# Delta heads with raw keys and queries: the lengths move into beta, the values and the head norm; the decay comes from one F32 tile; the score tiles are placed first

## The chip, the cores and the metric

The kernel runs on one core of a Trainium2 chip. The metric is the device time of one execution in microseconds (us). Five engines work side by side, each through its own instructions in order: TensorE (PE, matrix products), VectorE (DVE), ScalarE (ACT), GpSimd (POOL) and SyncE (SP), whose queue here issues all loads and stores. Semaphores order the engines among each other.

## The reference

One layer of an encoder over 1024 tokens of width 1024: a mixer, a cross-attention into 256 memory tokens, and a SwiGLU block, each with RMS norms before and after it. The mixer has two halves that read the same projection. One is a windowed softmax attention. The other, which the change touches, is a gated delta rule with 4 heads of width 128, in both directions of time:

```python
q = _l2norm(q) * DN_HEAD_K ** -0.5          # _l2norm(x) = x * rsqrt(sum(x*x) + EPS)
k = _l2norm(k)
g = jnp.cumsum(g, axis=-1)                  # within a chunk
decay = exp(where(incl, g[..., :, None] - g[..., None, :], -inf))
kb = k * beta[..., None]
lower = where(strict, einsum('bhnid,bhnjd->bhnij', kb, k) * decay, 0.0)
sol = triangular_solve(lower + eye(c), concat([v * beta, kb * exp(g)]))
qk = einsum('bhnid,bhnjd->bhnij', q, k) * decay
# per chunk: v_new = u - w @ state; o = qg @ state + qk @ v_new; state = state * gl + kg.T @ v_new
o = o_fwd + o_bwd
o = o * rsqrt(mean(o * o, axis=-1, keepdims=True) + EPS) * g_out * silu(gate)
```

q, k and v are a centred 5-tap convolution and SiLU of projected columns. The kernel uses chunks of 128 tokens.

## The kernel before

The kernel is written against a tile framework. Each engine's order is set by a scheduler that plays the program on its own model of times: a ready instruction that stands earlier in the program goes first. Buffers come from pools, and a new tile waits for the last readers of the memory that it takes.

The mixer has three stages. ORDER_1 takes the delta heads 0 to 3: `delta_proj` (D) projects the key, query and value columns of a head. Each projection is 48 matmuls of 128x512 (line 259; activation and weight are split into a high and a low part, F32R tiles) and is then convolved: ACT copies the product out of PSUM, DVE adds four taps (line 284, tile `acc`, a ring of 3), ACT applies SiLU. `prep` (P) makes of a head what the recurrence needs, in two halves of four chunks that take turns. `base_inverse` (B) inverts, for two heads at once, the 32x32 diagonal blocks of I + lower on DVE, 30 steps of two instructions (lines 524 and 526), after it has loaded the blocks (tile `V`, four loads) and the beta rows.

A half of `prep` goes like this. POOL spreads the gate over a mask, once for the gate's high part and once for its low part and for both directions (`gm`, line 450), and four F32R matmuls (line 451) sum them to exponents, of which ACT makes the decay `E`. PE turns the key tile (line 441) into PSUM, ACT squares it and sums, POOL takes the power -1/2 (lines 159 and 160), DVE multiplies (line 466): a key of length one, token by token, in `kv`. The query goes the same way. The values are turned and copied (line 468). Then PE turns the normed keys and queries back (line 473), ACT copies them (line 474), `kv` is stored to `d_kv` as one block of 1 MB, and PE makes the score products key by key and key by query (line 481), which DVE multiplies with `E` out of PSUM (`U`, line 484, stored to `d_u`; `pc`, line 488). All these PSUM results come from one ring of five banks, `ps`. Beta is turned, stored to `d_beta` once for all heads and read by both base inverses.

ORDER_2 takes the two `levels` for each pair of heads (they read what the base inverse stored, multiply it up to 128x128 and store `Z`), the gates (G), the attention projections (A, V) and the first attention windows (W). Its pools `tw` and `tl_` lie where those of ORDER_1 were. ORDER_3 runs the two recurrences (`scan`), step by step, beside windows and the memory's keys and values (K, V). A step loads `kv` and `pz`. From the fifth step on, the two directions are added, squared and normed with the power on POOL (`rstd_of`) and scaled by the gate.

The rest (output projection, cross-attention, SwiGLU) is not touched.

## Time and profile before

| what | us |
|---|---|
| median of three runs (1584.72 to 1590.94) | 1587.42 |
| the profiled execution, its own time | 1588.8 |
| span of the profiled execution, first to last instruction | 1587.1 |
| delta heads (70 to 255 us): length of the stretch / PE busy in it | 185 / 170.5 |
| levels of heads 0 and 1, second base inverse (255 to 345 us) | 90 / 79.1 |
| levels of heads 2 and 3, first windows (345 to 405 us) | 60 / 55.3 |
| recurrences, windows, memory (405 to 570 us) | 165 / 152.9 |

The profile names an instruction by line, engine, operation and tiles; buffer numbers are left out. A matmul with F32 operands of 128 columns shows as two records, a transpose and an F32R matmul as one. A record of PE lasts longer than the time to the next one's start, because matmuls overlap; what one costs in a row is read from start to start. `PEclk` is the share of TensorE's full clock that was granted. "Waited for" gives total time, number of waits and the longest, and the engine and line that ended them.

### The profile page before, as it was taken

What the parts mean: (1) busy time and instruction counts of PE and PEld (TensorE: products, weight loads), DVE (VectorE), ACT (ScalarE), POOL (GpSimd) and SP (SyncE); (2) the same over time, 40 slices, a digit from 0 to 9 for tenths busy, and PEclk for the clock granted to TensorE, in tenths of its full rate; (3) what the DMA queues carried; (4) which work ended last, traced back from release to release, by engine and by line L of the source; (5) the groups of instructions that cost most, each with busy time, mean ns of one, the idle gap of its engine ahead of it and who ended that gap; (6) DMA issues with size and microseconds to landing.
All of it is one profiled execution on the core that took longest, in us unless ns stands there. A gap on an engine that the chain in (4) does not pass through costs nothing.

```text
span 1587.1 us, 21186 instructions
## 1 busy us (share of the span) xinstructions
PE 1505.9 (95%) x7514; PEld 1260.3 (79%) x7514; DVE 1059.3 (67%) x1616; ACT 762.4 (48%) x1523; POOL 497.4 (31%) x447
## 2 busy tenths in 40 slices
PE   6999889989799989999999999999999999999998
PEld 5877777868689967788888777888888888888786
DVE  6846887975678865444345549677768655596565
ACT  6556543238766685554335566322322332344532
POOL 2368644233134510243301140443434433100021
PEclk9999999989999999999999999999999999999999
DMA  6134148483998675455222254443335332853354
GB/s 207 42 118 129 41 153 226 113 206 103 283 289 284 191 251 206 146 186 157 69 72 79 90 186 140 128 154 127 118 118 166 100 100 100 292 206 112 107 171 161
DMA packets 252151, 242.97 MB, mean 153 GB/s; under 512 B 33528, under 2 KB 187021, under 8 KB 252045
## 3 DMA queue, kind: packets, MB, share of 16 engines
q1 hardware_dynamic: 252045, 241.62, 48.0%
q8 instruction: 59, 0.97, 0.3%
q14 instruction: 47, 0.39, 0.1%
HBM read 172.07 MB, written 66.88 MB: 151 GB/s over the span
## 4 chain that ended last, share of the span: by engine, by line
PE 67%; DVE 13%; DMA 7%; ACT 5%; issue 3%; POOL 3%; SPq 2%; DVEq 0%; POOLq 0%; ACTq 0%
PE pmg L1005 8%; PE pD L1180 7%; PE pE L1180 7%; PE pA L1180 6%; PE pcq L259 6%; PE pdX L1370 5%; PE pg L259 4%; PE pdA L1370 4%; PE pB L1180 4%; PE psc L777 3%; DVE acc L284 2%; PE pdD L1370 2%; DVE tmpb L524 2%; DVE A L526 2%; PE pcs L1086 1%
## 5 line engine op out<-in xcount | busy, mean ns | idle before, releaser
L102 ACT CAST whi<-wraw 128x1024 fp32r<-128x1024 f32 x108 | 113.3, 1050 | 161.5 <-PE pmg L1005 34.9
L103 POOL TENSOR_TENSOR wlo<-wraw,whi 128x1024 fp32r<-128x1024 f32 x48 | 119.7, 2494 | 193.9 <-ACT whi L102 171.4
L259 PE MATMUL pg<-hlo,whi 128*128 128x512 f32 x352 | 140.2, 399 | 0.0
L259 PE MATMUL pg<-hhi,whi 128*128 128x512 f32 x352 | 140.1, 399 | 0.1
L259 PE MATMUL pg<-hhi,wlo 128*128 128x512 f32 x352 | 139.9, 398 | 0.0
L103 DVE TENSOR_TENSOR wlo<-wraw,whi 128x1024 fp32r<-128x1024 f32 x60 | 74.5, 1244 | 79.4 <-ACT whi L102 75.1
L1005 PE MATMUL pmg<-whi,b 128*128 128x512 f32 x384 | 118.4, 394 | 2.6 <-ACT whi L102 2.2
L1180 PE MATMUL pA<-s,whi 128*128 128x512 f32 x352 | 109.6, 392 | 1.4 <-ACT m L1197 1.4
L284 DVE SCALAR_TENSOR_TENSOR acc<-cp,cols,acc 128x1024 f32<-128x1024 f32 x48 | 73.8, 1539 | 19.5 <-ACT acc L282 18.9
L1005 PEld LDWEIGHTS pmg<-whi,b 128*128 128x128 f32 x384 | 71.2, 188 | 17.9 <-ACT whi L102 2.7
L259 PEld LDWEIGHTS pg<-hhi,whi 128*128 128x128 f32 x352 | 67.1, 191 | 13.6 <-ACT hhi L102 0.4
L1257 POOL TENSOR_TENSOR act<-act,up 128x512 f32<-128x512 f32 x33 | 50.1, 1519 | 88.1 <-DVE up L1256 53.0
L259 PEld LDWEIGHTS pg<-hhi,wlo 128*128 128x128 f32 x352 | 67.1, 191 | 13.2
L259 PEld LDWEIGHTS pg<-hlo,whi 128*128 128x128 f32 x352 | 67.2, 191 | 13.1
L1370 PE MATMUL pdX<-dhl,whi 128*128 128x512 f32 x264 | 76.1, 390 | 1.5 <-ACT dhl L102 0.8
L1180 PEld LDWEIGHTS pA<-s,whi 128*128 128x128 f32 x352 | 65.3, 188 | 15.2 <-ACT m L1197 2.0
L1400 POOL TENSOR_SCALAR frs<-sq 128x1 f32<-128x1 f32 x8 | 11.9, 1497 | 195.7 <-ACT jk L1389 194.8
L1005 PE MATMUL pmg<-wlo,b 128*128 128x512 f32 x192 | 71.4, 391 | 0.0
L1180 PE MATMUL pA<-s,wlo 128*128 128x512 f32 x176 | 68.8, 392 | 1.9 <-DVE wlo L103 1.9
L102 ACT CAST whi<-araw 128x1024 fp32r<-128x1024 f32 (+1 forms) x36 | 35.4, 982 | 71.3 <-PE pdX L1370 27.6
L1229 POOL TENSOR_TENSOR sr<-wraw 128x512 f32<-128x512 f32 x22 | 29.2, 1328 | 126.4 <-DMA wraw<-in_w_gate_up_dram 125.6
L103 DVE TENSOR_TENSOR wlo<-araw,whi 128x1024 fp32r<-128x1024 f32 (+1 forms) x36 | 40.7, 1132 | 38.5 <-ACT whi L102 38.3
(409 smaller groups left out, 4230.3 us busy)
## 6 DMA issues: line engine op xcount, KB each, us to landing
wraw<-in_w_gate_up_dram SPq DMA_DIRECT2D x52, 512.0 KB, 3.9
kv<-d_kv SPq DMA_DIRECT2D x32, 512.0 KB, 6.7
wraw<-in_w_in_dram SPq DMA_DIRECT2D x22, 512.0 KB, 4.3
b<-in_w_down_dram SPq DMA_DIRECT2D x20, 512.0 KB, 7.0
araw<-d_as SPq DMA_DIRECT2D x20, 512.0 KB, 3.7
d_kv<-kv SPq DMA_DIRECT2D x8, 1024.0 KB, 7.2
pz<-d_pz SPq DMA_DIRECT2D x32, 256.0 KB, 6.0
wraw<-in_w_ckv_dram SPq DMA_DIRECT2D x16, 512.0 KB, 7.2
```

The lines of the kernel that those rows point to most:

```text
L102: nc.scalar.copy(hi, src)
L103: (eng or nc.vector).tensor_tensor(lo, src, f32(hi), ALU.subtract)
L259: nc.tensor.matmul(p_, w[:, k, :], ah[a][:, k, :], start=(k == 0 and i == 0), stop=(k == nk - 1 and i == 2))
L284: nc.vector.scalar_tensor_tensor(acc, cp[:, t:t + S], taps[t], acc, ALU.mult, ALU.add)
L524: nc.vector.tensor_tensor(tv, A[:, j + 1:, j:j + 1].to_broadcast([P, n, j]), A[:, j:j + 1, 0:j].to_broadcast([P, n, j]), ALU.mult)
L526: nc.vector.tensor_tensor(A[:, j + 1:, 0:j], A[:, j + 1:, 0:j], tv, ALU.add)
L777: nc.tensor.matmul(out[:, d, h, :], lt[:, d, h, :], rt[:, d, h, :], start=True, stop=True)
L1005: nc.tensor.matmul(pp[t], act[a][:, k, tt], w_[:, kk, :], start=(k == 0 and i == 0), stop=(k == KT - 1 and i == 2))
L1180: nc.tensor.matmul(out_, w[a][:, k, :], xx[b_][:, k, :], start=(start and k == 0 and i == 0), stop=(k == HK - 1 and i == 2), skip_group_ch ...
L1229: nc.gpsimd.tensor_tensor(s[0], b_[:, 0:HK], b_[:, HK:], ALU.add)
L1257: nc.gpsimd.tensor_tensor(o_, o_, up, ALU.mult)
L1370: nc.tensor.matmul(banks[t], a[:, k - k0, tt], w, start=(first and k == 0 and i == 0), stop=(k == NB - 1 and i == 2), skip_group_check=not ...
```

## The change

Keys and queries stay raw. With x the sum of a key's squares plus EPS, the key by key products carry the lengths of two keys; beta is divided by x, the values are multiplied by the root of x, so that the recurrence gives the same result. The query's length and its 128 cancel in the head norm but for EPS, which is scaled by the query's squares instead (`epsq`).

So the two norm multiplies and the two turns back go. The raw key and query tiles (width by token, as they come from the convolution) are stored from `acc` straight to their places in `d_kv`, are the operands of the score products, and are still turned for their squares. `acc` becomes a ring of 5. The decay's exponents come from two F32 matmuls on the unsplit gate in place of four F32R ones. Beta is stored per pair of heads, after the second head's keys are squared. The norm of the recurrence's output takes one more POOL instruction. A line takes the eight score tiles as the first of the pool `tw`.

```diff
-    mU_r = sm.tile([P, P], F32R, name="mU_r")
-    mL_r = sm.tile([P, P], F32R, name="mL_r")
+    mU_s = sm.tile([P, P], F32, name="mU_s")
+    mL_s = sm.tile([P, P], F32, name="mL_s")
...
-        acc = tcv.tile([P, S], F32, tag="acc", name="acc", bufs=3)
+        acc = tcv.tile([P, S], F32, tag="acc", name="acc", bufs=5)
...
-    pt = small()
-    nc.tensor.transpose(pt[0:64, 0:P], beta.rearrange("p d h c -> p (d h c)"), ident)
-    bT = sm.tile([64, P], F32, name="bT")
-    nc.scalar.copy(bT, pt[0:64, 0:P])
-    nc.sync.dma_start(d_beta, bT)
+    phalf = sm.tile([P, 32], F32, name="phalf")
+    nc.gpsimd.memset(phalf, 0.5)
...
+    def beta_rows(g):
+        hs = slice(2 * g, 2 * g + 2)
+        bp = sm.tile([P, 2, 2, NT], F32, name=f"bp{g}")
+        xi = sm.tile([P, 2, NT], F32, name=f"xi{g}")
+        nc.vector.reciprocal(xi, xk[:, hs, :])
+        nc.vector.tensor_tensor(bp, beta[:, :, hs, :], bc(xi, 1, (P, 2, 2, NT)), ALU.mult)
+        pt = small()
+        nc.tensor.transpose(pt[0:32, 0:P], bp.rearrange("p d h c -> p (d h c)"), ident)
+        bT = t2.tile([32, P], F32, tag="bT", name="bT", bufs=1)
+        nc.scalar.copy(bT, pt[0:32, 0:P])
+        nc.sync.dma_start(d_beta[g], bT)
...
+        for src, i in ((kc, 2), (qc, 3)):
+            nc.sync.dma_start(d_kv[g][:, :, hh, i].rearrange("c p n -> p c n"), src.rearrange("p (c n) -> p c n", c=NT))
...
-                for part in (ghi, glo):
-                    gm = t2.tile([P, 4, P], F32R, tag="gm", name="gm")
-                    nc.gpsimd.tensor_tensor(gm, bc(part[:, d, h, c4], 2, (P, 4, P)), bc(cm[mi], 1, (P, 4, P)), ALU.mult)
-                    nc.tensor.matmul(pa, ml, gm.rearrange("p c n -> p (c n)"), start=(n == 0), stop=(n == 3))
-                    n += 1
+                gm = t2.tile([P, 4, P], F32, tag="gm", name="gm")
+                nc.gpsimd.tensor_tensor(gm, bc(G[:, d, h, c4], 2, (P, 4, P)), bc(cm[mi], 1, (P, 4, P)), ALU.mult)
+                nc.tensor.matmul(pa, ml, gm.rearrange("p c n -> p (c n)"), start=(d == 0), stop=(d == 1))
...
-                rs = t2.tile([P, 4], F32, tag="rs4", name="rs4", bufs=4)
-                rstd_of(rs, ss, n, e)
-                nc.vector.tensor_tensor(kv[:, :, i, :], pk, bc(rs, 2, (P, 4, P)), ALU.mult)
+            kv = t2.tile([P, 4, 2, P], F32, tag="kv", name="kv")
             yield
-            nc.scalar.copy(kv[:, :, 1, :], turned(vc))
-            for i, o in ((0, 2), (3, 3)):
-                yield
-                p_ = small()
-                for j in range(4):
-                    nc.tensor.transpose(p_[:, j * P:(j + 1) * P], kv[:, j, i, :], ident)
-                nc.scalar.copy(kv[:, :, o, :], p_.rearrange("p (c n) -> p c n", c=4))
-            nc.sync.dma_start(d_kv[g][c4, :, hh].rearrange("c p s n -> p c s n"), kv)
+            pk = turned(kc)
+            nc.scalar.copy(kv[:, :, 0, :], pk)
+            ss = squares(pk, False)
+            nc.gpsimd.tensor_scalar(xk[:, h, c4], ss, EPS, None, ALU.add)
+            nc.gpsimd.tensor_tensor(rootk[:, h, c4], xk[:, h, c4], phalf[:, 0:4], ALU.pow)
+            if hh and b:
+                beta_rows(g)
...
-                    nc.tensor.matmul(p_[:, j, :], kv[:, j, 2, :], kv[:, j, i, :], start=True, stop=True)
+                    o = (4 * b + j) * P
+                    nc.tensor.matmul(p_[:, j, :], kc[:, o:o + P], src[:, o:o + P], start=True, stop=True)
...
+            nc.gpsimd.tensor_scalar(epsq[:, g, :, 1 - b, hh], squares(turned(qc), b == 0), P * EPS, P * EPS * EPS,
+                                    ALU.mult, ALU.add)
+            yield
+            nc.vector.tensor_tensor(kv[:, :, 1, :], turned(vc), bc(rootk[:, h, c4], 2, (P, 4, P)), ALU.mult)
+            nc.sync.dma_start(d_kv[g][c4, :, hh, 0:2].rearrange("c p s n -> p c s n"), kv)
...
+    tw.tile([P, 384], F32, tag="sc", name="sc", bufs=8)
...
-            rstd_of(rs.rearrange("p d h -> p (d h)"), ss.rearrange("p d h -> p (d h)"), 1.0 / P, EPS)
+            nc.gpsimd.tensor_scalar(rf, sf, 1.0 / P, None, ALU.mult)
+            nc.gpsimd.tensor_tensor(rf, rf, epsq[:, g, step - NT // 2].rearrange("p d h -> p (d h)"), ALU.add)
+            nc.gpsimd.tensor_tensor(rf, rf, mhalf[:, 0:4], ALU.pow)
```

The scheduler orders the engines anew. Three places follow; a number behind a tile's name is that of its buffer.

The first is PE in the `prep` of head 1. Rows of line 259 are projections. Before, the turns back (line 473) stand between projections, and the score products (line 481) come after them:

```order
L473 MATMUL ps_1210<-ident_68,kv_1109 128x128 x4
L259 MATMUL pg_1354<-hhi1_227,whi_1349 128x512
L259 MATMUL pg_1354<-hlo1_228,whi_1349 128x512
L473 MATMUL ps_1216<-ident_68,kv_1125 128x128 x4
L259 MATMUL pg_1354<-hhi1_227,wlo_1350 128x512
L473 MATMUL ps_1222<-ident_68,kv_1109 128x128 x4
L473 MATMUL ps_1229<-ident_68,kv_1125 128x128 x4
L259 MATMUL pg_1422<-hhi0_141,whi_1418 128x512
```

After, in the same `prep` (line 435 turns the beta rows, 486 makes the score products, 452 turns the raw queries for their squares):

```order
L435 MATMUL ps_1107<-ident_68,bp0_1103 32x128
L486 MATMUL ps_1112<-acc_899 128x128 x4
L486 MATMUL ps_1120<-acc_899 128x128 x4
L486 MATMUL ps_1128<-acc_968,acc_899 128x128 x4
L486 MATMUL ps_1139<-acc_968,acc_899 128x128 x4
L452 MATMUL ps_1150<-ident_68,acc_968 128x128 x4
L259 MATMUL pg_1273<-hhi0_142,whi_1269 128x512
L259 MATMUL pg_1273<-hlo0_143,whi_1269 128x512
L452 MATMUL ps_1165<-ident_68,acc_968 128x128 x4
```

The sixteen score products now stand in one piece, and before the query is turned. Over the four heads, from the first `gm` product to the first level, the 540 projection matmuls stand in 18 stretches, where they stood in 44. The score products of head 1 come after 194 of the 540, where 236 stood ahead of the first of them.

The second is DVE inside the first base inverse, at the `prep` of head 2. Before (524 and 526 are a step of the inverse, 284 a tap, 484 and 488 take the score products out of PSUM):

```order
L524 TENSOR_TENSOR tmpb_2070<-A_2066 128x238
L284 SCALAR_TENSOR_TENSOR acc_1797<-cp_1794,cols_71,acc_1797 128x1024
L526 TENSOR_TENSOR A_2066<-A_2066,tmpb_2070 128x14x17
L484 TENSOR_TENSOR U_1640<-ps_1635,E_1514 128x512
L488 TENSOR_TENSOR pc_1648<-ps_1643,E_1498 128x512
```

After (536 and 538 are the step, 489 is `U`):

```order
L538 TENSOR_TENSOR A_1911<-A_1911,tmpb_1915 128x22x9
L489 TENSOR_TENSOR U_1466<-ps_1461,E_1414 128x512
L536 TENSOR_TENSOR tmpb_1915<-A_1911 128x210
L538 TENSOR_TENSOR A_1911<-A_1911,tmpb_1915 128x21x10
L489 TENSOR_TENSOR U_1474<-ps_1469,E_1424 128x512
L536 TENSOR_TENSOR tmpb_1915<-A_1911 128x220
```

The two `U` of head 2 have moved from behind steps 16 and 17 of the base inverse to behind steps 9 and 10.

The third is SP's queue at the start of the recurrences. Before, the last loads of the first stretch are:

```order
L785 DMA kv_4185<-d_kv1_100 128x1024
L786 DMA pz_4184<-d_pz11_104 128x512
L785 DMA kv_4418<-d_kv0_99 128x1024
L786 DMA pz_4417<-d_pz00_101 128x512
L676 DMA kraw_4236<-d_k_97 64x1024
L125 DMA wraw_4383<-in_w_ckv_dram 128x8x128
```

After (798 loads `kv`, 799 `pz`, 679 stores a window, 688 loads the attention's keys, 635 a window's queries):

```order
L799 DMA pz_4278<-d_pz10_103 128x512
L798 DMA kv_4279<-d_kv1_100 128x1024
L679 DMA d_mix_113<-ao_3345 64x4x128
L688 DMA kraw_4082<-d_k_97 64x1024
L125 DMA wraw_4229<-in_w_ckv_dram 128x8x128
L635 DMA qr_3872<-d_q_96 64x4x128 x2
```

Eight loads of `kv` and seven of `pz` now stand ahead of the attention's keys (`kraw`) and of the memory's weights, where five and five stood.

## The prediction

> **What bounds the kernel now.** I read the page's head first, then the stages, then who PE waited for, then the order of time at the places that the change touches.

> ```profile
> span 1587.1 us, 21186 instructions
> ...
> PE 1505.9 (95%) x7514; PEld 1260.3 (79%) x7514; DVE 1059.3 (67%) x1616; ACT 762.4 (48%) x1523; POOL 497.4 (31%) x447
> ...
> PE 67%; DVE 13%; DMA 7%; ACT 5%; issue 3%; POOL 3%; SPq 2%; DVEq 0%; POOLq 0%; ACTq 0%
> ```

> PE sets the end: it is busy for 95% of the span and is two thirds of the chain that ended last. A microsecond is worth something if it is taken from PE's work or from its waits. The change lies in the mixer, whose stages are (columns: stretch, length, busy time of PE, PEld, DVE, ACT, POOL with counts, granted clock, DMA share, GB/s):

> ```profile
> 70.00:255.00 185.00, 170.54 (x878) 141.69 (x878) 133.51 (x148) 99.92 (x253) 116.25 (x107) 0.98 0.41 121
> 255.00:345.00 90.00, 79.05 (x409) 67.36 (x409) 78.52 (x143) 22.79 (x53) 29.57 (x22) 0.93 0.63 166
> 345.00:405.00 60.00, 55.26 (x314) 47.59 (x313) 35.73 (x88) 45.26 (x100) 19.67 (x19) 0.96 0.47 136
> 405.00:570.00 165.00, 152.93 (x1125) 142.42 (x1126) 129.48 (x336) 115.06 (x306) 62.73 (x65) 0.97 0.82 253
> ```

> The delta heads take 185 us with 14.5 us in which PE stands; the next 90 us have 11 us of standing, with DVE at 87%. From 60 to 420 us PE waited for (engine, line, releaser: total, times, longest):

> ```profile
> PE ps L441 <- DVE kv L466: 5.5, 3, 2.6
> PE ps L583 <- DVE L L576: 5.0, 1, 5.0
> PE ps L473 <- DVE kv L466: 3.8, 3, 1.7
> PE ps L451 <- POOL gm L450: 2.9, 3, 1.5
> PE ps L574 <- DVE Z L606: 2.4, 1, 2.4
> PE ps L441 <- ACT E L454: 2.0, 1, 2.0
> ```

> Lines 441 and 473 wait for the norm multiply that the change takes out, 9.3 us in all. The 583 and 574 waits come in the levels, when DVE still works on the second base inverse.

> **PE's work.** What an instruction costs in a row is read from start to start (start, length, engine, line, operation, shape, count):

> ```profile
> 243.16 0.60 PE L473 MATMUL ps<-ident,kv 128*128 128x128 f32 x4
> 243.51 0.48 PE L259 MATMUL pg<-hhi,wlo 128*128 128x512 f32 x1
> 243.83 0.39 PE L259 MATMUL pg<-hhi,whi 128*128 128x512 f32 x1
> 244.06 0.40 PE L259 MATMUL pg<-hlo,whi 128*128 128x512 f32 x1
> ...
> 244.75 3.74 PE L481 MATMUL ps<-kv 128*128 128x128 f32 x32
> 248.25 0.48 PE L259 MATMUL pg<-hlo,whi 128*128 128x512 f32 x1
> ```

> Four turns take 243.51 - 243.16 = 0.35 us. Eight halves lose eight turns back each, 64 turns: 64 x 0.35 / 4 = 5.6 us less. An F32R matmul of 512 columns takes 244.06 - 243.83 = 0.23 us; eight halves lose four: 32 x 0.23 = 7.4 us less. In their place come 16 F32 matmuls of 512 columns, a shape that the trace does not have. Sixteen F32 matmuls of 128 columns (32 records) take 248.25 - 244.75 = 3.50 us, 0.219 each. If the time goes by columns, 512 take 4 x 0.219 = 0.875 us, 14.0 us in all, 6.6 more than the F32R ones. The lower end: F32 matmuls of 32 columns cost as much as those of 128, so what is paid there may be the weights and not the columns:

> ```profile
> 261.71 1.87 PE L583 MATMUL ps<-m,L 128*128 128x32 f32 x16
> 263.41 0.47 PE L259 MATMUL pg<-hhi,wlo 128*128 128x512 f32 x1
> ```

> Eight of them in 263.41 - 261.71 = 1.70 us, 0.21 each. Then two records of 512 columns would cost what two F32R matmuls do, 0.46 us, and the decay nothing more than before. I take 0.875: the same type on the same engine is the nearest row. Two turns of beta in place of one: 0.1 us. Work in sum: -5.6 + 6.6 + 0.1 = **+1.1 us** (-5.5 to +1.1); PE has no less to do than before.

> [...]

> Fewer pieces: the first projection after small matmuls takes 243.83 - 243.51 = 0.32 us to the next, 0.09 above 0.23. The order has 44 stretches of projections in the four heads before and 18 now: 26 x 0.09 = **-2.3 us** (0 to -2.3).

> **PE's waits in the heads.** The norm multiply goes, and with it 9.3 us; of the 2.9 us for `gm` I take half away, since POOL makes two of these tiles per half and not four: **-10.8 us** (-14.2 to 0). The wait for `E` stays. New waits come in, because five banks of `ps` must still be emptied: the turned query needs a bank that the squares on ACT release or `U` on DVE. The costs beside PE (busy us, mean ns):

> ```profile
> L463 ACT ACTIVATE jk<-ps 128x128 f32<-128x128 f32 x64 | 17.2, 333 | 0.0
> L474 ACT COPY kv<-ps 128x512 f32<-128x512 f32 x16 | 9.0, 603 | 1.5 <-PE ps L473 1.4
> L466 DVE TENSOR_TENSOR kv<-ps,rs 128x512 f32<-128x512 f32 x16 | 10.9, 687 | 17.4 <-POOL rs L160 15.7 <-POOL cp L276 0.9 <-POOL cp L277 0.7
> L160 POOL TENSOR_TENSOR rs<-rs,mhalf 128x4 f32<-128x4 f32 x16 | 19.1, 1200 | 0.5
> L646 POOL TENSOR_TENSOR es<-prm,m 128x4 f32<-128x4 f32 x9 | 2.2, 244 | 15.5 <-DVE m L636 8.8 <-PE ptw L657 6.4
> ```

> ACT loses two copies per half and DVE one multiply of 0.687 us (8 x 0.687 = 5.5 us), POOL half of its powers. I give the new waits 4 us, one per head, the size of two multiplies plus two copies (2.6 us) and a little queueing; between 0 and 9.3, the wait that the same banks cost until now. **+4 us**.

> **The base inverses.** They run on DVE and are hindered by POOL (`gm`, line 450):

> ```profile
> 226.39 0.24 DVE L526 TENSOR_TENSOR A<-A,tmpb 128x84 f32<-128x84 f32 x1
> 226.77 1.04 POOL L450 TENSOR_TENSOR gm<-ghi,C 128x512 fp32r<-128x512 f32 x1
> 226.92 0.96 DVE L526 TENSOR_TENSOR A<-A,tmpb 128x58 f32<-128x58 f32 x1
> 227.92 0.93 DVE L524 TENSOR_TENSOR tmpb<-A 128x30 f32<-128x30 f32 x1
> ```

> A step that takes 0.24 us takes 0.95 beside a `gm`: each of the eight `gm` that go in heads 2 and 3 frees up to 0.7 us of DVE there, 5.6 us at most. Besides, `U` of head 1 is made 42 projections earlier in PE's order, 42 x 0.23 = 9.7 us, and the first inverse starts from it (above its rows that of the taps, which stand between its steps):

> ```profile
> L284 DVE SCALAR_TENSOR_TENSOR acc<-cp,cols,acc 128x1024 f32<-128x1024 f32 x48 | 73.8, 1539 | 19.5 <-ACT acc L282 18.9
> 162.37 3.95 DVE L515 SCALAR_TENSOR_TENSOR A<-V,bB 64x1024 f32<-64x1024 f32 x1 [8.97 <-DMA V<-d_u]
> 229.19 2.12 DVE L528 TENSOR_TENSOR V<-A,bB 128x1024 f32<-128x1024 f32 x1
> 267.65 2.00 DVE L515 SCALAR_TENSOR_TENSOR A<-V,bB 64x1024 f32<-64x1024 f32 x1 [3.04 <-DMA V<-d_u]
> ```

> The second inverse should then start some 10 us earlier against PE, and the levels' waits of 5.0 and 2.4 us mostly go: **-6 us** (-7.4 to 0). Late next is the beta row: squares, reciprocal, turn, copy, store, load. It runs beside `U`, its store (6.1 us) and the `V` loads, so I cost it at nothing; without that cover a store and a load would follow that of `U`, up to 6.1 us each by the row of `d_u` below. The granted clock was 0.98 and 0.93 in these stretches: 2% of 185 and 7% of 90 us are 10 us, of which I take a fifth, **-2 us** (0 to -6).

> **Stores and loads.** `d_kv` was written as 1 MB and is now written as half a MB from `kv` and twice half a MB per head from `acc`:

> ```profile
> d_kv<-kv SPq DMA_DIRECT2D x8, 1024.0 KB, 7.2
> d_u<-U SPq DMA_DIRECT2D x8, 256.0 KB, 6.1
> kv<-d_kv SPq DMA_DIRECT2D x32, 512.0 KB, 6.7
> ```

> The bytes are the same, and DMA is 41% busy there: nothing. SP is in order, though: behind the store of a raw key, which waits for SiLU, stand weight loads; these are needed some 100 projections (23 us) later, so that is nothing too. At the start of the recurrences three `kv` and two `pz` more stand ahead of the attention's keys and the memory's weights: 3 x 0.52 + 2 x 0.26 = 2.1 MB, at 253 GB/s 8.3 us. PE waits there already, in the chain for these loads:

> ```profile
> 409.44 7.22 DMA pz<-d_pz
> 416.68 11.60 DMA kv<-d_kv
> ```

> I take **+2.5 us** (0 to 8.3), since the scan's own loads come sooner for it. One more POOL instruction of 0.244 us per norm is hidden for a step; the last ones are not: **+0.3 us**. The score tiles' place lets other tiles take memory that is free earlier or later; values no longer lie where the base inverse was, and I cost it at nothing.

> **Sum** against the profiled execution: 1588.8 + 1.1 - 2.3 - 10.8 + 4 - 6 - 2 + 2.5 + 0.3 = 1575.6 us. That execution is 1.4 above the median, so 1574.2 against 1587.4: 1574, or -0.8%. About 0.5%, 8 us, is what a measurement of this kernel tells from no change.

> **Rivals.** *DVE holds PE in the heads (slower).* `U` of head 2 now stands behind step 9 of the first inverse. If that inverse doesn't start earlier (the fourth `V` load is queued on SP behind the stores of `kv`), DVE is late for PE: 162.4, plus 6 us for the inverse's first two instructions, nine steps at twice some 0.6 us and four taps at 1.5 us make 185, while PE, which has lost some 10 us of waits, would be there at about 174. That is 11 us in head 2, and as much in head 3, whose beta row stands on DVE behind the inverse's end at 231. With 22 us in place of 4, and without the levels' 6, the sum is 1588.8 + 1.1 - 2.3 - 10.8 + 22 - 2 + 2.5 + 0.3 = 1599.6, 1598 against the median. From 11 us of new waits on the kernel gains nothing, from 19 it is slower by over 0.5%. Against it: DVE has less to do and `U` comes earlier.

> *The gain is given back (no change).* PE has no less work. If the levels still wait for the second inverse, the clock stays and the recurrences wait for all 8.3 us of loads, the sum is 1588.8 + 1.1 - 2.3 - 10.8 + 4 + 8.3 + 0.3 = 1589.4, 1588 against the median. For it: the later stages start from DVE's inverse and from loads, not from PE's work in the heads.

> *More goes.* The F32 matmuls cost the lower end (-5.5), all 14.2 us of waits go with 2 us new, then the levels' 7.4 and 6 us of clock, and the loads are hidden: 1588.8 - 5.5 - 2.3 - 14.2 + 2 - 7.4 - 6 + 0.3 = 1555.7, 1554 against the median.

> **Chances.** Forecast (1566 to 1579) 0.51; more (below) 0.12; given back (1580 to 1595) 0.19; DVE holds PE (above) 0.18. So faster by over 0.5% 0.63, within it 0.19, slower 0.18. The range reaches half way into "more" and to the price of the slower rival: 1559 to 1598, with some 0.06 left out below and 0.13 above.

> **What would show it.** The wait of lines 441 and 473 for `kv` gone from PE's list, waits for `U`, `pc` or squares of about 4 us in its place; `gm` products of 0.875 us; the first inverse starting before 155 us; the level of head 2 on PE before 322 us where it came at 330; the 405 to 570 stretch as long as before, 10 to 15 us earlier. Waits above 15 us for DVE in the heads, or an inverse that starts at 162, would make the forecast wrong.

## The result: no change

The changed kernel takes 1586.85 us (median of 20 runs, 1581.95 to 1591.49), the kernel before 1587.01 us (20 runs, 1582.54 to 1590.94). The ratio is 0.9996 (95% interval 0.9988 to 1.0004). 1574 us was forecast. The profiled execution of the changed kernel is the fastest of its 20 (1581.95 us), that of the kernel before lies 1.8 us above its median: the 7 us between the two pages are scatter for the most part.

The head of the changed kernel's page, and its chain by engine:

```profile
span 1580.1 us, 21010 instructions
...
PE 1503.9 (95%) x7451; PEld 1256.4 (80%) x7451; DVE 1047.9 (66%) x1609; ACT 748.8 (47%) x1504; POOL 462.1 (29%) x432
...
PE 74%; DVE 11%; DMA 6%; ACT 4%; issue 2%; SPq 1%; POOL 1%; DVEq 0%; POOLq 0%; ACTq 0%
```

VectorE has lost 11 us, ScalarE 14, GpSimd 35; PE 2. By stage, in the columns of the prediction's table:

```profile
70.00:255.00 185.00, 171.83 (x831) 137.90 (x829) 128.02 (x143) 91.72 (x237) 86.33 (x84) 0.98 0.44 123
255.00:345.00 90.00, 79.88 (x405) 68.09 (x405) 77.56 (x154) 25.55 (x60) 27.93 (x22) 0.91 0.64 160
345.00:405.00 60.00, 56.70 (x319) 48.16 (x318) 34.28 (x85) 43.84 (x106) 17.51 (x20) 0.97 0.48 143
405.00:570.00 165.00, 155.04 (x1158) 145.17 (x1156) 134.09 (x345) 120.09 (x315) 62.01 (x72) 0.98 0.86 266
```

PE is as busy in the heads as before (170.5, now 171.8 us of 185), and the clock of the second stretch fell from 0.93 to 0.91. Whom PE waited for from 60 to 420 us:

```profile
PE ps L595 <- DVE L L588: 6.2, 2, 3.9
PE ps L460 <- POOL gm L459: 4.9, 2, 3.7
PE ps L486 <- DVE U L489: 3.6, 1, 3.6
...
PE ps L586 <- DVE Z L618: 3.1, 1, 3.1
PE ps L586 <- DMA Ul<-d_u: 2.0, 2, 1.8
...
PE ps L452 <- DVE U L489: 1.1, 1, 1.1
PE ps L486 <- ACT E L462: 0.8, 1, 0.8
PE ps L435 <- DVE bp L433: 0.7, 1, 0.7
PE psc L790 <- DMA pz<-d_pz: 0.6, 1, 0.6
```

The waits for `kv` are gone (9.3 us). In their place stand waits for `gm` (4.9 us, before 2.9) and for `U` (4.7, before 0.3), and the levels still wait: for `L`, `Z` and `Ul` 11.3 us.

**Where the difference can lie.** The first turn of the cross-attention's norm (line 974 before, 990 now, tile `ptn`) stands in the first half of the output projection, behind all that the change touches. From it on, both kernels take the same time: 1587.1 - 672.46 = 914.6 us and 1580.1 - 665.43 = 914.7 us (first row of the kernel before, second of the changed one).

```profile
672.46 1.03 PE L974 MATMUL ptn<-ident,xr 128*128 128x128 f32 x8
```

```profile
665.43 1.03 PE L990 MATMUL ptn<-ident,xr 128*128 128x128 f32 x8
```

So what counts is the stretch from 70 us to that turn (called the norm turn below), and for each kernel one row gives its length and PE's busy time in it. First the kernel before, then three executions with PE's order of the changed kernel: its own profile, and those of two experiments below, no_score_place (PE's order the same row by row) and half_decay_same_work (the same but for which decay product comes first).

```profile
70.00:672.50 602.50, 551.72 (x3136) 472.96 (x3136) 434.04 (x783) 345.88 (x816) 239.54 (x229) 0.97 0.60 181
```

```profile
70.00:665.40 595.40, 549.64 (x3074) 469.01 (x3073) 423.26 (x779) 331.74 (x796) 204.01 (x212) 0.96 0.61 182
```

```profile
70.00:670.50 600.50, 553.53 (x3075) 471.27 (x3074) 424.38 (x779) 332.39 (x797) 204.71 (x212) 0.96 0.61 180
```

```profile
70.00:671.10 601.10, 553.21 (x3077) 471.69 (x3077) 422.48 (x779) 332.98 (x798) 204.81 (x213) 0.96 0.60 180
```

Before: 551.7 busy + 50.8 idle. After: 549.6 + 45.8, 553.5 + 47.0, 553.2 + 47.9; in the mean 552.1 + 46.9. PE's idle time fell by 3.9 us and its busy time not at all. These are one execution against three; the kernel before was profiled in one alone.

**Where the busy time comes from.** In windows of 1 us the granted clock is 1.00 or 0.50, except where a piece begins or ends, and half clock comes in pieces of 3.41 us or a multiple of it (6.83 and 10.24 us in the kernel before, from 278.14 and 339.58 us). In each of these executions the pieces lie on one grid of 3.41 us. Here is that grid, first of the kernel before around 189 us, then of the changed one around 176 and 217 us (columns as above):

```profile
186.03:189.45 3.42, 0.66 (x4) 0.42 (x4) 3.42 (x5) 2.77 (x4) 3.18 (x5) 0.99 0.00 0
189.45:192.86 3.41, 3.12 (x11) 2.63 (x12) 3.41 (x5) 0.00 (x0) 2.30 (x2) 0.51 0.01 2
192.86:196.27 3.41, 3.41 (x23) 2.96 (x22) 3.27 (x9) 3.27 (x5) 0.13 (x2) 1.00 0.02 5
```

```profile
172.71:176.12 3.41, 0.31 (x2) 0.00 (x0) 3.31 (x6) 2.29 (x3) 1.13 (x3) 0.99 0.00 0
176.12:179.54 3.42, 2.89 (x14) 2.89 (x15) 2.06 (x5) 3.39 (x14) 1.34 (x2) 0.51 0.26 77
...
213.67:217.08 3.41, 0.20 (x1) 0.00 (x0) 3.37 (x3) 2.44 (x3) 3.41 (x2) 0.99 0.87 193
217.08:220.50 3.42, 2.89 (x6) 1.71 (x7) 3.38 (x2) 0.00 (x0) 2.46 (x2) 0.51 0.95 307
```

Behind these windows, in which PE worked for 0.66, 0.31 and 0.20 us and stood for the rest, the next one ran at half clock (0.51). Before, PE stood there for `E` and `kv` (2.03 and 2.58 us). In the changed kernel it is `U` (3.63 us) and `gm` (3.74 us), the two new waits:

```profile
176.65 0.58 PE L486 MATMUL ps<-acc 128*128 128x128 f32 x1 [3.63 <-DVE U L489]
```

```profile
217.61 2.08 PE L460 MATMUL ps<-gm,mL_s 128*128 128x512 f32 x2 [3.74 <-POOL gm L459]
```

At half clock a projection took 191.93 - 191.51 = 0.42 us to the next, at full clock 194.17 - 193.94 = 0.23 (the kernel before):

```profile
191.51 0.63 PE L259 MATMUL pg<-hhi,whi 128*128 128x512 f32 x1
191.93 0.63 PE L259 MATMUL pg<-hlo,whi 128*128 128x512 f32 x1
...
193.94 0.39 PE L259 MATMUL pg<-hhi,whi 128*128 128x512 f32 x1
194.17 0.40 PE L259 MATMUL pg<-hlo,whi 128*128 128x512 f32 x1
```

By an estimate from the granted clock, a window at half clock costs half of its 3.41 us, 1.7 us, if PE has work for all of it. What a window costs at that price is called its loss below. Up to the norm turn the kernel before has 10 of them (a loss of 17.0 us), the three executions of the changed order 13, 14 and 15 (22.1, 23.8 and 25.5 us). The mean granted clock says the same over all runs: 0.9866 before (132 runs), 0.9840 after (20), and 0.0026 of 1585 us is 4.1 us. That is the full price. Over the 326 runs of this study, those of one kernel against each other, 0.001 of clock goes with 0.56 us (standard error 0.06), by which an estimate for 0.0026 is 1.5 us. That would fit if part of the half-clock time falls where PE would have waited anyhow.

The added windows don't lie behind the two new waits, since the kernel before has two in the heads as well:

| stretch | idle before | idle now (mean of three) | half-clock windows before | now (each of the three) |
|---|---|---|---|---|
| 70 to 255 us | 14.5 | 12.8 | 2 | 2, 2, 2 |
| 255 to 405 us | 15.7 | 13.9 | 5 | 6, 6, 7 |
| 405 to 570 us | 12.1 | 10.3 | 3 | 2, 3, 3 |
| 570 us to the norm turn | 8.6 | 9.9 | 0 | 3, 3, 3 |

Most of them came behind 570 us, in the memory's last values and the start of the output projection (the kernel before, then the changed one):

```profile
570.00:672.46 102.46, 93.89 (x416) 73.86 (x414) 56.77 (x70) 62.82 (x105) 11.32 (x18) 1.00 0.61 215
```

```profile
570.00:665.43 95.43, 86.22 (x366) 69.69 (x367) 49.34 (x55) 50.56 (x82) 10.22 (x17) 0.95 0.56 193
```

There PE waits 2.2 us for a weight of the memory's values and 2.8 us for ScalarE's copy of them (`vv`), where it waited 0.7 and 1.1 us before. No run tests why.

The window ahead need not be empty: behind 0.66 us of work in 3.42 us (the kernel before, from 186.03 us) the next one ran at half clock.

### The profile page after: what moved, and what is told of

It reads as the page before. It is cut to its first block, busy times and chain, and to the rows that moved or that the text cites. A ratio compares the mean times of both kernels' runs of the same rounds, so it can differ in the third digit from the quotient of the medians.

```text
span 1580.1 us, 21010 instructions
## 1 busy us (share of the span) xinstructions
PE 1503.9 (95%) x7451; PEld 1256.4 (80%) x7451; DVE 1047.9 (66%) x1609; ACT 748.8 (47%) x1504; POOL 462.1 (29%) x432
## 4 chain that ended last, share of the span: by engine, by line
PE 74%; DVE 11%; DMA 6%; ACT 4%; issue 2%; SPq 1%; POOL 1%; DVEq 0%; POOLq 0%; ACTq 0%
PE pmg L1021 10%; PE pD L1196 7%; PE pE L1196 7%; PE pg L259 7%; PE pA L1196 6%; PE pcq L259 6%; PE pdX L1386 5%; PE pdA L1386 4%; PE pB L1196 4%; PE psc L790 3%; DVE acc L284 3%; PE pdD L1386 2%; PE pcs L1102 1%; PE pco L1128 1%; PE pck L921 1%
## 5 line engine op out<-in xcount | busy, mean ns | idle before, releaser
L259 PE MATMUL pg<-hhi,whi 128*128 128x512 f32 x352 | 141.0, 401 | 0.0
L259 PE MATMUL pg<-hhi,wlo 128*128 128x512 f32 x352 | 140.8, 400 | 0.0
L259 PE MATMUL pg<-hlo,whi 128*128 128x512 f32 x352 | 140.3, 399 | 0.0
L284 DVE SCALAR_TENSOR_TENSOR acc<-cp,cols,acc 128x1024 f32<-128x1024 f32 x48 | 77.2, 1610 | 19.2 <-ACT acc L282 14.0
L259 PEld LDWEIGHTS pg<-hhi,whi 128*128 128x128 f32 x352 | 67.2, 191 | 14.4 <-issue 0.7
L259 PEld LDWEIGHTS pg<-hlo,whi 128*128 128x128 f32 x352 | 67.1, 191 | 14.2 <-issue 1.0
L259 PEld LDWEIGHTS pg<-hhi,wlo 128*128 128x128 f32 x352 | 67.4, 191 | 13.6 <-issue 0.5
L1416 POOL TENSOR_SCALAR frs<-sq 128x1 f32<-128x1 f32 x8 | 11.9, 1497 | 195.5 <-ACT jk L1405 194.6
## 6 DMA issues: line engine op xcount, KB each, us to landing
wraw<-in_w_gate_up_dram SPq DMA_DIRECT2D x52, 512.0 KB, 3.9
kv<-d_kv SPq DMA_DIRECT2D x32, 512.0 KB, 7.3
wraw<-in_w_in_dram SPq DMA_DIRECT2D x22, 512.0 KB, 4.7
b<-in_w_down_dram SPq DMA_DIRECT2D x20, 512.0 KB, 6.8
araw<-d_as SPq DMA_DIRECT2D x20, 512.0 KB, 3.7
pz<-d_pz SPq DMA_DIRECT2D x32, 256.0 KB, 7.1
wraw<-in_w_ckv_dram SPq DMA_DIRECT2D x16, 512.0 KB, 7.6
wraw<-in_w_out_dram SPq DMA_DIRECT2D x16, 512.0 KB, 4.1
```

What stands on the lines that cost most here:

```text
L259: nc.tensor.matmul(p_, w[:, k, :], ah[a][:, k, :], start=(k == 0 and i == 0), stop=(k == nk - 1 and i == 2))
L284: nc.vector.scalar_tensor_tensor(acc, cp[:, t:t + S], taps[t], acc, ALU.mult, ALU.add)
```

## The experiments

The theories as their expectations name them. A: PE's own work sets the time, and the F32 decay products took back what the removed turns gave. B: PE waits for VectorE's inverses and for loads, so that its work in the heads is covered. C: the place of the score tiles cost the gain. D: the half-clock windows behind long waits took it.

**The price of the decay products.** gm_back_to_r makes the decay as the kernel before does:

```diff
-            for d, (mi, ml) in enumerate((("mUi", mL_s), ("mLi", mU_s))):
-                gm = t2.tile([P, 4, P], F32, tag="gm", name="gm")
...
+            for d, (mi, ml) in enumerate((("mUi", mL_r), ("mLi", mU_r))):
+                for part in (ghi, glo):
+                    gm = t2.tile([P, 4, P], F32R, tag="gm", name="gm")
...
```

> The changed kernel with the decay made as before: four F32R products of 512 columns from two parts of g in place of two F32 products; the rest of the change stays. Theory A (PE's work is what counts; the F32 products took back what the removed turns gave): PE has 16 x 0.85 - 32 x 0.23 = 6.2 us less than in the changed kernel, so 0.996 of it, ratio to before 0.992 to 0.997, with gm waits a little longer because POOL makes twice as many. Theory B (the levels wait for the second base inverse on DVE and the scan for its loads, so PE's work in the heads is hidden): ratio 0.998 to 1.002, PE's waits for L, Z and Ul in the levels grow by about the 6 us.

Measured: 0.9997 (0.9988 to 1.0007), clock 0.9819. The ratio is the one of theory B, but the waits for `L`, `Z` and `Ul` did not grow (10.0 us, 11.3 in the changed kernel). gm_f32_alone is the same edit the other way round, in the kernel before:

> The kernel before with the F32 decay products alone. Theory A: 6.2 us more work, less some 2 us of waits for gm: ratio 1.003 to 1.004. Theory B: ratio 0.998 to 1.002.

Measured: 1.0034 (1.0022 to 1.0046); 558.4 busy + 44.8 idle. PE's busy time rose by 6.7 us, where the prediction had 6.6, and 5.4 us of it were paid, as theory A has it. gm_doubled adds work:

```diff
+                if d == 0:
+                    nc.tensor.matmul(pa, ml, gm.rearrange("p c n -> p (c n)"), start=True, stop=True)
+                    nc.tensor.matmul(pa, ml, gm.rearrange("p c n -> p (c n)"), start=True, stop=True)
```

> The changed kernel with two idle F32 products of 512 columns more in each half head (16 in all, their result is overwritten): 16 x 0.85 = 13.7 us more of PE's work in the heads. Theory A: 1.0080 of the changed kernel (1.006 to 1.009 with waits hidden under it). Theory B: less than 1.003, since the levels' waits shrink by it.

Measured: 1.0030 (1.0017 to 1.0043), 5.4 us for 13.7 us of work. That is 1.0034 of the changed kernel, under A's range and at the upper edge of B's. So neither A nor B holds alone: added work is paid in part, and work taken away from the changed kernel gave nothing. The rest of the change without the F32 products is worth nothing either (gm_back_to_r against the kernel before), so their price is not what ate the gain.

**The place of the score tiles.** no_score_place drops the line that allocates `sc` first.

> The changed kernel without the line that places the score tiles first. Theory A and B: same as the changed kernel, ratio to before 0.998 to 1.001. Theory C (the place of the score tiles makes the attention's or the scan's first tiles wait for memory, and that gave the gain back): ratio 0.993 to 0.997, with the scan's first score earlier.

Measured: 0.9990 (0.9979 to 1.0001). C falls; PE's order is the same with and without the line.

**Waits one at a time.** fill_waits keeps PE busy where it waits:

```diff
+            if h == 3 and b == 0:
+                fill(pa, 14)
...
+                if h < 2 and b == 0 and w == 32:
+                    fill(p_, 14 if h == 0 else 9)
```

> The changed kernel with idle F32R products of 512 columns (0.23 us each, their result is overwritten) put directly ahead of three products that wait in it: 14 ahead of the first decay product of head 3 (waited 3.74 us for gm), 14 and 9 ahead of the first level product of heads 0 and 1 (waited 3.93 and 2.28 us for L). 37 x 0.23 = 8.5 us more work for PE. Theory D (a wait that empties more than half of a 3.41 us window of PE's clock brings a window at half clock behind it; the gain of the change went into these): the half-clock windows at 217, 264 and 302 us go, 4 to 5 of 1.7 us, the mean granted clock rises from 0.984 to 0.987 or more, and the ratio to before is 0.995 to 0.998. Rival (the work is what counts): 1.001 to 1.005, clock as in the changed kernel.

Measured: 1.0028 (1.0018 to 1.0039), clock 0.9852. The clock rose by 0.0012, where D expected 0.003, and the time rose too, as its rival has it. From the waits of this kernel (L444 is the idle product):

```profile
PE ps L444 <- DVE L L596: 5.8, 2, 3.1
...
PE ps L494 <- DVE U L497: 3.6, 1, 3.6
PE ps L468 <- POOL gm L467: 3.4, 3, 1.6
```

The idle products ahead of the levels stand behind the same wait as the levels: the PSUM bank that they need is the one that VectorE frees when it has made `L`. So 23 of the 37 were plain work (23 x 0.23 = 5.3 us; by the ratios the kernel is 5.1 us behind the changed one), and the run doesn't decide on D. A fill in a bank of its own wasn't tried.

inverse_on_dve moves the last product of the base inverse from GpSimd, where head 3's decay tiles stand behind it, to VectorE:

```diff
-        nc.gpsimd.tensor_tensor(A, A, bc(bB, 2, (P, 32, 32)), ALU.mult)
+        nc.vector.tensor_tensor(A, A, bc(bB, 2, (P, 32, 32)), ALU.mult)
```

> The changed kernel with the last product of the base inverse (A times beta, 128 x 1024) on VectorE in place of GpSimd. In the changed kernel the decay tiles of head 3 stand behind it on GpSimd and PE waits 3.74 us for them, with a half-clock window (1.7 us) behind. If such single long waits take the gain: ratio to before 0.996 to 0.998, the wait for gm under 1 us. If another wait takes its place (VectorE has 2 x 2 us more): 0.999 to 1.001.

Measured: 1.0025 (1.0013 to 1.0036), slower than either expectation. The wait for `gm` goes from 4.9 to 1.4 us, and two others take more than that:

```profile
PE ps L435 <- DVE bp L433: 7.9, 2, 7.2
...
PE psw L646 <- POOL qs L638: 4.2, 1, 4.2
...
PE ps L460 <- POOL gm L459: 1.4, 1, 1.4
```

half_inverse runs the inverse's loop as `range(1, 31, 2)`:

> The changed kernel with every second step of the two base inverses left out (15 of 30 steps each, so the inverses are wrong): some 10 us less of VectorE in each. Theory B (PE waits in the levels and heads for VectorE, which works on the inverses): the waits for L, Z and U (13 us) shrink to under 5, with 3 to 5 half-clock windows less, ratio 0.991 to 0.995. Theory A (PE's own work bounds): 0.998 to 1.000.

Measured: 1.0027 (1.0014 to 1.0040). VectorE has 18 us less to do up to the norm turn (404.8 against 423.3 us busy) and PE idles longer, 52.6 us. Its waits for `L`, `Z` and `U` are 9.4 us (14.0 in the changed kernel), not under 5. B in this plain form falls: less of VectorE's work on the inverses made the kernel no faster. The planner, which sees the shorter loop, gives PE another order, so the run doesn't hold the rest fixed. Why it is slower by some 5 us stays open.

**A product left out.** half_decay drops the second direction:

```diff
-            for d, (mi, ml) in enumerate((("mUi", mL_s), ("mLi", mU_s))):
+            for d, (mi, ml) in enumerate((("mUi", mL_s),)):
```

> The changed kernel without the second direction of the decay (one F32 product of 512 columns per half head in place of two, and one decay tile on GpSimd; so it leaves out half of the exponent). PE has 16 x 0.85 / 2 = 6.8 us less, GpSimd 8 tiles less. Theory A (PE's work in the heads counts): ratio 0.995 to 0.996. Theory B (it is covered by waits for VectorE and by the clock): 0.997 to 1.000, longer waits for U and the levels, mean clock at or under 0.983.

Measured: 0.9862 (0.9844 to 0.9880): 21 us less for 6.8 us of work, more than any theory had. decay_tile_kept gives GpSimd its work back:

> As half_decay (second F32 decay product of each half head left out, so half of the exponent is missing), but GpSimd still makes the second decay tile, which nothing reads. PE's order is the one of half_decay row by row; the two kernels differ only in 8 tiles of 1.04 us on GpSimd, beside which a VectorE step of 0.24 us takes 0.95. If GpSimd's tiles hold the heads: ratio to before 0.993 to 1.000. If it is PE's 6.8 us and the order that comes with them: 0.985 to 0.989.

Measured: 0.9870 (0.9855 to 0.9885). GpSimd's tiles are not it. half_decay_same_work gives PE its work back, in the order of the changed kernel but for which direction comes first, and keeps the numbers:

```diff
-            for d, (mi, ml) in enumerate((("mUi", mL_s), ("mLi", mU_s))):
+            for d, (mi, ml) in reversed(tuple(enumerate((("mUi", mL_s), ("mLi", mU_s))))):
...
-                nc.tensor.matmul(pa, ml, gm.rearrange("p c n -> p (c n)"), start=(d == 0), stop=(d == 1))
+                nc.tensor.matmul(pa, ml, gm.rearrange("p c n -> p (c n)"), start=True, stop=True)
```

> The changed kernel with both F32 decay products made, but the first one (second direction) overwritten by the other: PE's order and work are those of the changed kernel, the numbers those of half_decay (half of the exponent is missing). If half_decay was fast because of its numbers (granted clock): ratio to before 0.987 to 0.992. If it was fast because of its order and its 6.8 us less work: 0.998 to 1.001, as the changed kernel.

Measured: 0.9993 (0.9985 to 1.0002). The numbers are not it. What is left is PE's order with its 6.8 us less work; the row of half_decay up to its norm turn:

```profile
70.00:648.70 578.70, 541.68 (x3058) 463.47 (x3057) 419.38 (x779) 324.54 (x791) 196.03 (x204) 0.97 0.62 187
```

Against half_decay_same_work that is 11.5 us less busy and 10.9 us less idle time (37.0 against 47.9); it has 11 half-clock windows where that has 15. Most of it is won in the heads: PE is at the first level at 234.75 us and not at 256.09, with 20 projections fewer ahead of it (4.6 us), the 6.8 us of products and 6.9 us of idle time where 13.4 stood. The waits for `gm`, 5.5 of these 13.4 us, are gone.

**Who makes the decay tiles.** decay_on_act has them made on ScalarE, decay_split every second one, r_decay_on_act all of gm_back_to_r's:

```diff
-                nc.gpsimd.tensor_tensor(gm, bc(G[:, d, h, c4], 2, (P, 4, P)), bc(cm[mi], 1, (P, 4, P)), ALU.mult)
+                for c in range(4):
+                    nc.scalar.activation(gm[:, c, :], cm[mi], AF.Identity, scale=G[:, d, h, 4 * b + c:4 * b + c + 1])
```

> The changed kernel with the decay tiles made on ScalarE (four scaled copies of 128 columns each, 64 in all, some 0.27 us each) in place of GpSimd; nothing is left out. If GpSimd's tiles hold the heads (its work blocks VectorE's steps of the inverse and is late for PE): the waits for gm go, ratio to before 0.990 to 0.996. If PE's work and the clock bound: 0.998 to 1.001. If ScalarE (50% busy in the heads) is late with E or the squares: over 1.002.

> The changed kernel with the second direction's decay tile on ScalarE and the first on GpSimd. Between the changed kernel and decay_on_act if the engine that makes the tiles counts: 0.993 to 0.998; otherwise 0.998 to 1.002.

> gm_back_to_r with all its decay tiles on ScalarE (128 scaled copies, some 34 us there): PE has 6.2 us less than the changed kernel and GpSimd 16 tiles less. If both PE's work and GpSimd's tiles count: 0.988 to 0.994. If the clock takes it back as in gm_back_to_r: 0.998 to 1.000, mean clock at or under 0.982. If ScalarE becomes late: over 1.002.

Measured: 1.0001 (0.9989 to 1.0013), 1.0003 (0.9994 to 1.0013), 0.9997 (0.9988 to 1.0005). Which engine makes the tiles makes no difference to the time. But the wait for `gm` didn't go with GpSimd's work: in decay_on_act a scaled copy took 0.40 us and not 0.27 (ScalarE was busy for 354.0 us up to the norm turn, for 331.7 in the changed kernel), and PE waited 4.8 us for `gm` from ScalarE.

**Where the decay stands in PE's order.** With two buffers for `gm`, the second half's tiles can't be made before the first half's are used. The planner therefore puts 20 projections (26 in head 3) between the two halves' products, and the keys' turns and products of the head come behind those. decay_four_deep changes only that:

```diff
-                gm = t2.tile([P, 4, P], F32, tag="gm", name="gm")
+                gm = t2.tile([P, 4, P], F32, tag="gm", name="gm", bufs=4)
```

> The changed kernel with four buffers for the decay tiles in place of two; nothing is left out. With two, the second half's products can't be made before the first half's are used: PE's order has 20 projections (4.6 us) between the two pairs, and 26 in head 3, and the keys' turns and products behind them. With four, all four products stand together, as the two of half_decay did, and the first level stands behind 718 projections and not 745. If this order is what made half_decay fast: ratio to before 0.988 to 0.994. If not: 0.998 to 1.002.

Measured: 1579.37 us, 0.9955 (0.9943 to 0.9967): with all of the work, a version faster than both kernels, though by less than expected if this order were all that made half_decay fast. Its row up to the norm turn and some of its waits up to 420 us:

```profile
70.00:662.50 592.50, 549.88 (x3076) 468.81 (x3075) 423.58 (x779) 326.86 (x793) 205.90 (x213) 0.97 0.61 183
```

```profile
PE ps L486 <- ACT E L462: 8.5, 2, 5.7
PE ps L595 <- DVE L L588: 4.2, 2, 2.9
PE ps L601 <- ACT bs L597: 4.0, 1, 4.0
...
PE ps L586 <- DVE Z L618: 0.3, 1, 0.3
...
PE ps L586 <- DMA Ul<-d_u: 0.2, 1, 0.2
```

Idle time is 42.6 us in place of 46.9, and the waits for `Z` and `Ul` are nearly gone. This profile has 12 half-clock windows, where the changed order had 13 to 15; but over its five runs the clock is 0.9838, no higher than the changed kernel's 0.9840, so the clock doesn't explain the gain. New is the wait for `E`, which now has four products ahead of it. The same depth elsewhere (r_decay_four_deep gives gm_back_to_r four buffers, and two for `pm`, for room):

> gm_back_to_r with four buffers for its decay tiles (and two in place of three for the masked products, for room). A half still needs four F32R products, so the second half's stand 26 projections behind the first's; PE has 6.2 us less than decay_four_deep, and the first level stands behind 739 projections (767 in gm_back_to_r). If order and work both count: 0.986 to 0.994. If only the halves standing together counts: 0.997 to 1.001.

> The kernel before with four buffers for its decay tiles. Its halves' products move apart by a stretch of 20 to 26 projections either way, and the first level stands behind 769 projections in place of 729. If the place of the levels in PE's order counts: 1.001 to 1.006. If depth alone frees GpSimd and PE: 0.994 to 0.998.

Measured: 0.9971 (0.9960 to 0.9982) and 1.0018 (1.0006 to 1.0030). The first is in the range expected if only the place of the halves counts. So depth alone is no gain; in the kernel before the time rose, as was expected there from the 769 projections ahead of the levels. decay_ahead takes the decay out of the head's start:

```diff
-ORDER_1 = "D0 P0 D1 P1 D2 P2 D3 P3 B0 B1".split()
+ORDER_1 = "E0 D0 P0 E1 D1 P1 E2 D2 P2 E3 D3 P3 B0 B1".split()
...
-            E = t2.tile([P, 4, P], F32, tag="E", name="E")
-            nc.scalar.activation(E, pa.rearrange("p (c n) -> p c n", c=4), AF.Exp)
+            E = Es[h, b]
```

> The changed kernel with the decay of a head (tiles, F32 products and exponential) issued ahead of the head's projections and no longer at the head's start; nothing is left out, two buffers as before. The products then stand inside the stretch of projections, the turns and products of a head follow without gm or E between them, and the first level stands behind 735 projections (745 in the changed kernel, 718 in decay_four_deep). If it is the decay at the head's start that holds the gain back: ratio to before 0.989 to 0.995, waits for gm and E under 2 us. If only the place of the levels counts: 0.996 to 0.999. If the gain of decay_four_deep was an accident of the order: 0.999 to 1.002.

> The same with the decay from four F32R products, as in gm_back_to_r: the order of everything else is that of decay_ahead row by row in its counts (first level behind 735 projections, the scan behind 341.1 - 6.2 us of work). If PE's 6.2 us count once the order is held: 0.0039 below decay_ahead, 0.985 to 0.991. If the clock or GpSimd's 16 tiles more take them back: within 0.0015 of decay_ahead.

Measured: 0.9970 (0.9958 to 0.9983) and 0.9988 (0.9978 to 0.9998). Moving the decay gains 4 us, most of what the depth did. That is in the range expected if only the place of the levels counts, and not in the one (0.989 to 0.995) for the decay at the head's start holding the gain back; the waits for `gm` and `E` are 3.3 us, not under 2. PE's 6.2 us less in the F32R version gain nothing here either. That holds in three pairs now: 0.9997 against 0.9996, 0.9971 against 0.9955, 0.9988 against 0.9970. The F32R version leaves PE more waits for tiles, as decay_ahead's and r_decay_ahead's rows show:

```profile
PE ps L450 <- POOL gm L449: 2.5, 1, 2.5
```

```profile
PE ps L458 <- POOL gm L457: 6.7, 7, 3.2
PE ps L504 <- ACT E L461: 5.5, 1, 5.5
```

The kernels side by side (us from 70 us to the norm turn in the profiled execution; projections ahead of the first level in PE's order):

| kernel | ratio | stretch = busy + idle | projections |
|---|---|---|---|
| before | 1 | 602.5 = 551.7 + 50.8 | 729 |
| changed (mean of three) | 0.9996 | 599.0 = 552.1 + 46.9 | 745 |
| gm_back_to_r | 0.9997 | 596.0 = 549.0 + 47.0 | 767 |
| gm_f32_alone | 1.0034 | 603.2 = 558.4 + 44.8 | 697 |
| decay_four_deep | 0.9955 | 592.5 = 549.9 + 42.6 | 718 |
| decay_ahead | 0.9970 | 594.3 = 549.3 + 45.0 | 735 |
| half_decay | 0.9862 | 578.7 = 541.7 + 37.0 | 725 |

The number of projections doesn't order the ratios by itself: half_decay (725) is faster than decay_four_deep (718), gm_f32_alone (697) slower than before. What makes half_decay's order so good, beyond its 6.8 us, stays open: no kernel with all the work had that order.

## Why the prediction was wrong

The norm's waits for `kv` went as forecast, and three terms failed. The wait for `gm` was to fall by half and rose by 2.0 us. The levels' waits were to lose 6 us and gained 1.5. The clock was to give 2 us and took some 1.5 to 4.1.

**The decay products: right.** 0.875 us was taken for an F32 product of 512 columns. In the changed kernel one takes 78.38 - 77.53 = 0.85 us:

```profile
77.53 1.02 PE L460 MATMUL ps<-gm,mL_s 128*128 128x512 f32 x2
78.38 0.49 PE L452 MATMUL ps<-ident,acc 128*128 128x128 f32 x3
```

Sixteen are 13.6 us, where 14.0 stood. gm_f32_alone's 6.7 us of busy time agree with the 6.6 us of the term; the sum for PE's work (+1.1, -2.3) is within what the rows can tell.

**The waits in the heads (-10.8, +4): wrong by half, through `gm`.** The 9.3 us for `kv` went. But `gm` was to keep half of its 2.9 us and took 4.9, because head 3's tiles stand on GpSimd behind the end of the first inverse:

```profile
212.84 2.73 POOL L541 TENSOR_TENSOR A<-A,bB 128x1024 f32<-128x1024 f32 x1 [3.04 <-DVE V L540]
215.54 4.00 POOL L459 TENSOR_TENSOR gm<-G,C 128x512 f32<-128x512 f32 x2
```

This inverse came earlier, as forecast, and so came ahead of those tiles in GpSimd's order; that the tiles were fewer didn't help them. `U`, `E`, `pc` and `bp` take 6.6 us, of which `E` and `U` had 2.3 before: 4.3 us are new, where 4 was given. In the heads the waits named went from 14.5 us (`kv` 9.3, `gm` 2.9, `E` 2.0, `U` 0.3) to 11.5: 3.0 us less, where 6.8 was the net of the two terms. Of the 3.8 us between, `gm` is 3.5.

**The base inverses (-6): the step was right, its worth was not.** The first inverse starts at 153.8 us (forecast: before 155) and the second 22 us earlier than before, at 245.5 where it was 267.65:

```profile
153.81 2.06 DVE L527 SCALAR_TENSOR_TENSOR A<-V,bB 64x1024 f32<-64x1024 f32 x1 [2.32 <-DMA V<-d_u]
```

```profile
245.53 2.07 DVE L527 SCALAR_TENSOR_TENSOR A<-V,bB 64x1024 f32<-64x1024 f32 x1 [7.18 <-DMA V<-d_u]
```

But PE came to the first level when it had before (254.22, now 254.33 us), since the planner put 745 projections ahead of it and not 729. So the second inverse's first steps, which stood 13 us behind PE's first level, stand 9 us ahead of it, and its steps lie between the `L` of the first levels on VectorE. Before, PE waited for `L` in the last levels; now it waits in the first ones, and for `Z` ahead of head 2 as before (first row of the kernel before, the others of the changed one):

```profile
341.84 3.59 PE L583 MATMUL ps<-m,L 128*128 128x32 f32 x16 [5.04 <-DVE L L576]
```

```profile
265.24 3.59 PE L595 MATMUL ps<-m,L 128*128 128x32 f32 x16 [3.93 <-DVE L L588]
301.88 3.27 PE L595 MATMUL ps<-m,L 128*128 128x32 f32 x16 [2.28 <-DVE L L588]
332.04 0.66 PE L586 MATMUL ps<-ident,Ul 128*128 128x128 f32 x4 [3.09 <-DVE Z L618]
```

The levels' waits (lines 574 to 589 before, 586 to 601 now) were 10.4 us and are 11.9; those for `L` moved from the last levels to the first ones, and the one for `Z` grew from 2.4 to 3.1 us. The level of head 2 came at 332.0 us, where it came at 330.2 and was forecast before 322. The prediction read the earlier `U` as time won against a PE that stays where it was, and left the planner out. That the inverse's steps are what delays `L` is read from VectorE's order; half_inverse, which halves them, changed PE's order too and doesn't show it.

**The granted clock (-2): wrong in sign.** It was costed as a fifth of the 10 us that the clock takes from the two stretches, as if fewer microseconds of waiting meant more clock. In these rows what counts is whether a wait, or several close together, empties most of a window: the waits of 3.6 and 3.7 us in the heads do, but so did those of 2.0 to 2.6 us there before. In the profiles the heads have two half-clock windows either way, and the added ones lie later, most of them behind 570 us. The clock fell by 0.0026, which is an estimated +1.5 to +4.1 us and not -2. Why the later waits became longer stays open.

**The scan's loads (+2.5), the norm's POOL instruction (+0.3): not seen.** PE's wait for `pz` fell from 2.0 to 0.6 us, and from the norm turn on the two kernels agree within 0.1 us. The score tiles' place was rightly costed at nothing.

**The sum.** Waits: -10.0 (-10.8, +4, -6, +2.5, +0.3) was forecast, -3.9 us of idle time is shown. Work and clock: -3.2 was forecast, +0.4 us of busy time is shown. -3.5 us from these profiles and -0.2 us from the medians lie 3.3 us apart; runs of one kernel scatter by 2 to 3 us (standard deviation), and only one profile of the kernel before stands against them. In time this is the rival "the gain is given back", and it rightly had the levels still waiting; its 8.3 us for the loads were not what gave the gain back. The slower rival had 22 us of new waits in heads 2 and 3. The one for `U` in head 2 came, with 3.6 us in place of 11; in head 3 the beta row (`bp`) took 0.7 us, and the 3.7 us there are for `gm`, which the rival didn't name. decay_four_deep and decay_ahead show that the place of the decay in PE's order, with its buffers, held back 4 to 6.5 of the missing 13 us, the work being the same; for the rest no experiment shows the cause. That the clock took 1.5 to 4.1 us is read from rows and runs, and no experiment here moved the clock alone.

## What to carry to other kernels

A wait that is taken from an in-order engine is worth only what the planner does with the freed time: read in the new order how much work stands ahead of the next wait, and which buffers hold the first steps of a stage apart (four buffers for `gm` in place of two gained 6.5 us in the changed kernel and lost 2.9 us in the kernel before). Read PE's waits by their lengths too and not by their sum alone, and look at what they leave of each clock window: a wait of 3.6 us, or two of 2.0 and 2.6 us with little work between them, emptied one here, which shorter and scattered waits don't have to. An experiment that changes work under a planner changes its order as well; a pair that holds one of them (half_decay and decay_tile_kept with PE's order the same row by row, decay_ahead and r_decay_ahead with the first level behind as many projections) says more than any run by itself.
